# Shift and weight of the first LayerNorm moved behind the transposes of a two-layer decoder trunk

## Chip, cores and metric

One core of a Trainium2 chip. The metric is device time in microseconds of one execution, as the median of several runs. All arithmetic is float32; products are made of two-part splits of float32 (below).

## What is computed

512 tokens of width 2048 pass two layers, each followed by a LayerNorm of the residual sum:

```
x1  = layer_norm(alpha * x  + s5_mixer(x),  ln_g[0], ln_b[0])
kv  = shared_kv(x1)
out = layer_norm(alpha * x1 + nsa_mixer(x1, kv), ln_g[1], ln_b[1])

def layer_norm(x, g, b):
    mu, var = mean(x), mean((x - mu)**2)          # over the 2048 channels of a token
    return (x - mu) * rsqrt(var + 1e-5) * g + b
```

The change is in how `x1` comes from layer 0 to layer 1. `x1` is needed twice: transposed (channels on the partitions, for every projection of layer 1) and as it is (the residual of the last LayerNorm).

## The kernel before

Every float32 operand of a matmul is split into a rounded high part and a rest (`split`: a copy on ScalarE, a subtraction on VectorE), and a product is three matmuls: high by high, high by rest, rest by high (`mm3`, lines 235 to 237). Weights come in units of 512 KB through SP's queue, in the order of use, and are split ahead of their use by `Weights` (ScalarE line 78, VectorE line 85, or GpSimd line 85 for the units in `pool_units`).

The phases are: layer 0 (`layer0_in`), its output projection with the first LayerNorm and the turn (`project_out` with `turn=True`), layer 1's projections and attention (`layer1_in`), and the output projection with the second LayerNorm (`project_out` with `turn=False`). One instruction stream for each engine is written by hand; there is no scheduler. Work beside the matmuls is written as generators in a `Background`: each `yield n` says how many ticks later its next piece may be issued, and each `mm3` of the main loop is three ticks in layer 0's projection (1.5 in the first projections of layer 1).

The tokens are four tiles `t` of 128. In `project_out`, the last column step goes tile by tile, 24 matmuls of 512 columns each. When a tile's last product is done, `add` (lines 939 and 940) adds the residual and takes statistics, and `finish(t)` normalises the tile's four blocks of 128x512:

- lines 950 to 968: mean and variance, a square root on ScalarE, one Newton step on VectorE (instructions of one column).
- by the table `LN_HOW`, a block is "d" (VectorE, lines 958 and 971, two operations with the broadcast weight `gb` and shift `bb`), "p" (ScalarE line 976, then weight and shift on GpSimd, lines 977 and 978) or "m" (VectorE 958, ScalarE 973, GpSimd 974).
- line 992 stores the finished tile to DRAM as `x1_d`, the later residual.
- lines 998 to 1002: per block, four transposes on TensorE into `tp` (two buffers), a copy to `x1h` on ScalarE, a subtraction to `x1l` on VectorE.

After it, still in `project_out`, the first two projections of layer 1 start with half of the tokens (tiles 0 and 1) while tiles 2 and 3 are still turned, then do the other half; line 1065 copies their results to `first`. The four weight units of these projections are split on GpSimd.

Of the kernel before, what the change touches and what calls it, by code (L numbers as in the profile page):

```python
# [891 lines left out]
def project_out(c, sc, u0, steps, K, yh, yl, prep, x_res, ln_g, ln_b, x_out, turn):  # L892
# [54 lines left out]
    fg = FG[turn]  # L947

    def finish(t):
# [3 lines left out]
        vs, gs, bs = ([z[:, cc * 512:cc * 512 + 512] for cc in range(4)] for z in (v[:, t], gb, bb))  # L953
        how = LN_HOW[turn][t]
        late = []
        early = [cc for cc in range(4) if how[cc] != "p"]
        for i, cc in enumerate(early):
            V.scalar_tensor_tensor(vs[cc], vs[cc], mv[:, t, 0:1], gs[cc], OP.subtract, OP.mult)  # L958
            if i % 2:
                yield fg[0]  # L960
            if i == (len(early) - 1 if turn else 1):

                V.reciprocal(r, r)
                V.tensor_scalar(q, mv[:, t, 1:2], LN_EPS, r, OP.add, OP.mult)
                V.tensor_scalar(q, q, r, -0.5, OP.mult, OP.mult)
                V.tensor_scalar(r, q, 1.5, r, OP.add, OP.mult)
                if "p" in how:
                    V.tensor_scalar(nb, mv[:, t, 0:1], r, -1.0, OP.mult, OP.mult)
        for cc in sorted(range(4), key=lambda cc: "pmd".index(how[cc])):
            if how[cc] == "d":  # L970
                V.scalar_tensor_tensor(vs[cc], vs[cc], r, bs[cc], OP.mult, OP.add)
            elif how[cc] == "m":
                S.activation(vs[cc], vs[cc], AF.Copy, scale=r)
                P.tensor_tensor(vs[cc], vs[cc], bs[cc], OP.add)
            else:
                S.activation(vs[cc], vs[cc], AF.Identity, scale=r, bias=nb)
                P.tensor_tensor(vs[cc], vs[cc], gs[cc], OP.mult)
                P.tensor_tensor(vs[cc], vs[cc], bs[cc], OP.add)
            if not turn:
                o = x_out[t, :, cc * 512:cc * 512 + 512]  # L980
                if how[cc] == "d":
                    SP.dma_start(o, vs[cc])
                elif POUT:
                    P.dma_start(o, vs[cc])
                else:
                    late.append((o, vs[cc]))
            yield fg[1]
        if not turn:
            for o, z in late:
                SP.dma_start(o, z)  # L990
            return
        SP.dma_start(x_out[t], v[:, t])
        yield fg[2]
        ts = slice(t * 128, t * 128 + 128)
# [648 lines left out]
```

## Time and profile before

| | us |
|---|---|
| median of three runs (1800.74 to 1807.41) | 1804.71 |
| the profiled execution | 1800.29 |
| its span on the core | 1798.4 |
| TensorE busy in the span | 1744.9 |
| VectorE, ScalarE, GpSimd busy | 1002.6, 604.8, 177.3 |

Times in the rows are microseconds from the span's start. Engines are PE (TensorE), PEld (its weight loads), DVE (VectorE), ACT (ScalarE), POOL (GpSimd) and SP (SyncE, which only issues DMAs). In a row of a timeline stand start, duration, engine, line, operation, result<-inputs and size; xN joins N instructions that follow each other, and a bracket tells how long the engine had been idle before and what released it.

### The profile page before, as it was taken

Reading aid. Unit: us, or ns where it says so; the run is one execution under the profiler, and the core shown is the slowest. Engines: PE = TensorE matmul, PEld = TensorE weight load, DVE = VectorE, ACT = ScalarE, POOL = GpSimd, SP = SyncE. Lnnn points to the kernel's source line nnn. Section 1 sums busy time; section 2 is a strip of 40 time slices with the busy share of each in tenths; the row PEclk is TensorE's granted clock in tenths of the full one; section 3 lists DMA queues with packets and bytes.
Section 4 is the critical chain, followed back from the end, with each engine's and each line's share of the span. In section 5 each row is a group of like instructions: output and inputs, shape, how many; then the busy total and the mean of one; then the engine's idle time right before and its main releaser. Section 6 shows DMA issues by size and latency. Waiting matters only on the chain.

```text
span 1798.4 us, 21845 instructions
## 1 busy us (share of the span) xinstructions
PE 1744.9 (97%) x8455; PEld 1448.5 (81%) x8455; DVE 1002.6 (56%) x1815; ACT 604.8 (34%) x1018; POOL 177.3 (10%) x233
## 2 busy tenths in 40 slices
PE   8899998997999999999999999999999999999997
PEld 6678887886788888888888888888888888888886
DVE  7678865548333455653555553555543555665346
ACT  3344434314333333332333332333332333333120
POOL 4911100006000000000000000000000000010000
PEclk9899999999999999999999999999999999999999
DMA  6477874544233322222222222222222222236343
GB/s 227 137 191 197 214 175 133 198 142 154 88 118 117 106 80 79 77 88 82 89 76 83 81 83 94 88 77 88 72 87 94 88 77 83 77 128 231 122 140 105
DMA packets 89752, 209.70 MB, mean 117 GB/s; under 512 B 25265, under 2 KB 34721, under 8 KB 88625
## 3 DMA queue, kind: packets, MB, share of 16 engines
q1 hardware_dynamic: 81008, 181.31, 31.1%
q0 software_dynamic: 6336, 22.81, 5.2%
q10 hardware_dynamic: 2304, 4.20, 0.6%
q8 instruction: 66, 1.08, 0.3%
q14 instruction: 38, 0.30, 0.1%
HBM read 188.42 MB, written 19.86 MB: 116 GB/s over the span
## 4 chain that ended last, share of the span: by engine, by line
PE 81%; DVE 3%; ACT 1%; issue 0%; DVEq 0%; ACTq 0%
PE ps L235 23%; PE ps L237 23%; PE ps L236 23%; PE tp L1447 2%; PE s L237 1%; PE s L235 1%; PE s L236 1%; PE o L236 1%; PE o L237 1%; DVE v L958 1%; PE o L235 1%; PE cps L1212 1%; PE tp L1412 0%; PE o L1421 0%; DVE x1l L1002 0%
## 5 line engine op out<-in xcount | busy, mean ns | idle before, releaser
L235 PE MATMUL ps<-x1h,hl 128*128 128x512 f32 (+1 forms) x1440 | 563.7, 391 | 1.6 <-ACT hl L78 1.6
L237 PE MATMUL ps<-x1h,hl 128*128 128x512 f32 (+1 forms) x1440 | 556.7, 387 | 0.5 <-DVE hl L85 0.5
L236 PE MATMUL ps<-x1l,hl 128*128 128x512 f32 (+1 forms) x1440 | 555.7, 386 | 0.0
L85 DVE TENSOR_TENSOR hl<-wr,hl 128x1024 fp32r<-128x1024 f32 (+1 forms) x247 | 301.0, 1222 | 312.2 <-ACT hl L78 308.2
L78 ACT CAST hl<-wr 128x1024 fp32r<-128x1024 f32 (+1 forms) x273 | 284.4, 1045 | 220.4 <-PE ps L237 182.6
L237 PEld LDWEIGHTS ps<-x1h,hl 128*128 128x128 f32 x1440 | 270.5, 188 | 57.2 <-DVE hl L85 1.0
L235 PEld LDWEIGHTS ps<-x1h,hl 128*128 128x128 f32 x1440 | 271.0, 188 | 48.3 <-ACT hl L78 1.8
L236 PEld LDWEIGHTS ps<-x1l,hl 128*128 128x128 f32 x1440 | 271.1, 188 | 46.3
L1384 ACT ACTIVATE p<-s,m 128x384 f32<-128x384 f32 (+3 forms) x128 | 67.6, 528 | 357.6 <-DVE m L1383 357.6
L1320 POOL TENSOR_TENSOR y<-y,z 128x512 f32<-128x512 f32 x32 | 41.5, 1296 | 999.8 <-DVE z L1319 863.0
L241 DVE TENSOR_TENSOR pl<-tp,ph 128x512 fp32r<-128x512 f32 (+3 forms) x128 | 61.9, 487 | 110.0 <-ACT ph L240 109.6
L237 PE MATMUL ps<-xh,hl 128*128 128x512 f32 x256 | 104.0, 406 | 11.4 <-DMA hl<-w_in_b 11.4
L235 PE MATMUL ps<-xh,hl 128*128 128x512 f32 x256 | 109.8, 429 | 5.4 <-ACT xh L787 5.4
L236 PE MATMUL ps<-xl,hl 128*128 128x512 f32 x256 | 103.5, 404 | 2.6 <-DVE xl L788 2.6
L240 ACT CAST ph<-tp 128x512 fp32r<-128x512 f32 (+3 forms) x128 | 54.0, 426 | 151.2 <-PE tp L1447 150.9
L235 PE MATMUL ps<-hl,y1h 128*128 128x512 f32 x256 | 99.7, 389 | 0.0
L236 PE MATMUL ps<-hl,y1h 128*128 128x512 f32 x256 | 99.6, 389 | 0.0
L237 PE MATMUL ps<-hl,y1l 128*128 128x512 f32 x256 | 99.6, 389 | 0.0
L237 PEld LDWEIGHTS ps<-xh,hl 128*128 128x128 f32 x256 | 50.1, 196 | 23.9 <-DMA hl<-w_in_b 12.6
L1383 DVE TENSOR_REDUCE m<-s 128x1 f32<-128x384 f32 (+3 forms) x128 | 62.8, 491 | 4.4
L1306 DVE SCALAR_TENSOR_TENSOR z<-z,ps 128x512 f32<-128x512 f32 x48 | 33.0, 687 | 57.1 <-ACT z L1305 57.0
L235 PEld LDWEIGHTS ps<-xh,hl 128*128 128x128 f32 x256 | 50.3, 197 | 16.1 <-ACT xh L787 5.6
(350 smaller groups left out, 2306.8 us busy)
## 6 DMA issues: line engine op xcount, KB each, us to landing
wr<-b_w_in SPq DMA_DIRECT2D x128, 512.0 KB, 3.2
wr<-kv_w SPq DMA_DIRECT2D x48, 512.0 KB, 3.2
wr<-b_w_out SPq DMA_DIRECT2D x32, 512.0 KB, 3.4
wr<-w_in_b SPq DMA_DIRECT2D x24, 512.0 KB, 5.1
hl<-w_in_b POOLq DMA_DIRECT2D x22, 512.0 KB, 7.1
wr<-w_out SPq DMA_DIRECT2D x16, 512.0 KB, 3.6
xr<-xT SPq DMA_DIRECT2D x16, 256.0 KB, 4.3
Tz<-k_d SPq DMA_DIRECT2D x64, 64.0 KB, 4.2
```

The lines of the kernel that those rows point to most:

```text
L78: self.nc.scalar.copy(h[:, :n], r[:, :n])
L85: eng.tensor_tensor(l[:, :n], r[:, :n], h[:, :n].bitcast(F32), OP.subtract)
L235: PE.matmul(o, sh, mh, start=start, stop=False)
L236: PE.matmul(o, sh, ml, start=False, stop=False)
L237: PE.matmul(o, sl, mh, start=False, stop=stop)
L240: self.nc.scalar.copy(h, src)
L241: self.nc.vector.tensor_tensor(l, src, h.bitcast(F32), OP.subtract)
L1306: self.nc.vector.scalar_tensor_tensor(z, z, 1.0, ps, OP.add, OP.mult)
L1320: P.tensor_tensor(y[0], y[0], z, OP.add)
L1383: self.nc.vector.tensor_reduce(m[:, b - 1, i:i + 1], s, AX.X, OP.max, negate=True)
L1384: self.nc.scalar.activation(self.p[h, b][i], s, AF.Exp, bias=m[:, b - 1, i:i + 1], accum_out=self.sums[h, b][:, i:i + 1])
L1447: PE.transpose(tp[:, 128 * (i - j):128 * (i - j) + 128], p[i][:, at:at + 128], ident)
```

## The change

The normalised tile is made without weight and shift: (x - mean) / deviation, two blocks on VectorE and two on ScalarE, nothing on GpSimd. It is transposed in this form, and as a row of the transposed tile is one channel, weight and shift are then one number per partition. Each of the four 128x128 pieces of a block gets them on its way from `tp` into a new tile `xt` (three buffers): pieces 0 and 2 on ScalarE, 1 and 3 on VectorE. The split into `x1h` and `x1l` reads `xt`. The store to DRAM goes to a new tensor `xn_d` and holds the normalised tile; a new generator `residual`, in the fourth lane of the next phase, loads it block by block through GpSimd's queue, multiplies and adds on GpSimd, and stores it to `x1_d`. The gaps of the generators change as well.

```diff
         with yscope, ExitStack() as sc:
             xh, xl = project_out(c, sc, index["w_out"], OUT0, KE, yh, yl, lambda k: None, A["x"], A["ln_g"][0],
-                                 A["ln_b"][0], x1_d, True)
+                                 A["ln_b"][0], xn_d, True)
         with ExitStack() as sc:
-            y = layer1_in(c, sc, seq, xh, xl, y_d)
+            y = layer1_in(c, sc, seq, xh, xl, y_d, xn_d, x1_d)
...
-    gb = st.tile([128, D], F32, name="gb")
-    bb = st.tile([128, D], F32, name="bb")
-    P.dma_start(gb, ln_g.partition_broadcast(128))
-    P.dma_start(bb, ln_b.partition_broadcast(128))
+    if turn:
+        gbT = st.tile([128, 2, KD], F32, name="gbT")
+        P.dma_start(gbT, c.A["ln0"])
...
+    def finish_turn(t):
+        V.bn_aggr(mv[:, t], stats[:, t])
+        r, q, nb = (rs[:, t, i:i + 1] for i in range(3))
+        S.activation(r, mv[:, t, 1:2], AF.Sqrt, bias=eps)
+        inverse(t)
+        V.tensor_scalar(nb, mv[:, t, 0:1], r, -1.0, OP.mult, OP.mult)
+        vs = [v[:, t, cc * 512:cc * 512 + 512] for cc in range(4)]
+        ts = slice(t * 128, t * 128 + 128)
+        for cc in range(4):
+            if LN_ACT[cc]:
+                S.activation(vs[cc], vs[cc], AF.Identity, scale=r, bias=nb)
             else:
-                S.activation(vs[cc], vs[cc], AF.Identity, scale=r, bias=nb)
-                P.tensor_tensor(vs[cc], vs[cc], gs[cc], OP.mult)
-                P.tensor_tensor(vs[cc], vs[cc], bs[cc], OP.add)
...
+                V.tensor_scalar(vs[cc], vs[cc], mv[:, t, 0:1], r, OP.subtract, OP.mult)
+        yield TG[0]
         for cc in range(4):
             tp = pt.tile([128, 4, 128], F32, name="tp")
             for i in range(4):
                 PE.transpose(tp[:, i], vs[cc][:, i * 128:i * 128 + 128], ident)
+            x = st.tile([128, 4, 128], F32, tag="xt", name="xt", bufs=3)
+            for i in range(4):
+                g, b = (gbT[:, j, 4 * cc + i:4 * cc + i + 1] for j in range(2))
+                if i in XT_ACT:
+                    S.activation(x[:, i], tp[:, i], AF.Identity, scale=g, bias=b)
+                else:
+                    V.tensor_scalar(x[:, i], tp[:, i], g, b, OP.mult, OP.add)
             h, l = (z[:, 4 * cc:4 * cc + 4, ts] for z in (xh, xl))
-            S.copy(h, tp)
-            yield fg[3]
-            V.tensor_tensor(l, tp, h.bitcast(F32), OP.subtract)
+            S.copy(h, x)
+            yield TG[1]
+            V.tensor_tensor(l, x, h.bitcast(F32), OP.subtract)
             turned[t] += 1
+        SP.dma_start(x_out[t], v[:, t])
...
-FG = {True: (9, 1, 9, 6), False: (4, 3)}
-LN_HOW = {True: ('pddp', 'dppd', 'mdmm', 'dmmm'), False: ('dddd', 'dddd', 'dddd', 'dddd')}
+FG = (4, 3)
+TG = (6, 6)
+LN_ACT = (0, 1, 0, 1)
+XT_ACT = (0, 2)
...
+def residual(c, pool, xn_d, x1_d):
+    P = c.nc.gpsimd
+    for half in range(2):
+        g, b = (pool.tile([128, 1024], F32, tag=n, name=n) for n in ("g0", "b0"))
+        hs = slice(half * 1024, half * 1024 + 1024)
+        P.dma_start(g, c.A["ln_g"][0][hs].partition_broadcast(128))
+        P.dma_start(b, c.A["ln_b"][0][hs].partition_broadcast(128))
+        for t in range(4):
+            for i in range(2):
+                cs, here = (slice(lo, lo + 512) for lo in (half * 1024 + i * 512, i * 512))
+                x = pool.tile([128, 512], F32, tag="xn", name="xn", bufs=2)
+                P.dma_start(x, xn_d[t, :, cs])
+                yield RGAP
+                P.tensor_tensor(x, x, g[:, here], OP.mult)
+                P.tensor_tensor(x, x, b[:, here], OP.add)
+                P.dma_start(x1_d[t, :, cs], x)
+                yield RGAP
+RGAP = 18
...
     at.kc_tiles(0, cp)
+    bg.add(3, residual(c, cp, xn_d, x1_d))
```

How the instructions stand. First ScalarE from the first transposed block of tile 0 on, before; `tp_N` is a block's transposes in the order of their numbers, and a bracket names the engines whose semaphores the instruction waits for:

```order
L1000 CAST x1h_2744<-tp_3251 128x4x128 [waits PE_49]
L976 ACTIVATE v_2732<-v_2732,rs_2735 128x512 [waits DVE_49]
L1000 CAST x1h_2744<-tp_3272 128x4x128 [waits PE_49]
L976 ACTIVATE v_2732<-v_2732,rs_2735 128x512
L1000 CAST x1h_2744<-tp_3289 128x4x128 [waits PE_49]
```

And in the changed kernel, the first two blocks (lines of the changed file: 987 a piece, 991 the copy to `x1h`):

```order
L987 ACTIVATE xt_3218<-tp_3213,gbT_2729 128x128 [waits DMASW4_49,PE_49]
L987 ACTIVATE xt_3218<-tp_3213,gbT_2729 128x128 [waits DVE_49]
L991 CAST x1h_2743<-xt_3218 128x4x128 [waits DVE_49]
L987 ACTIVATE xt_3236<-tp_3231,gbT_2729 128x128 [waits DMASW5_49,PE_49]
L987 ACTIVATE xt_3236<-tp_3231,gbT_2729 128x128 [waits DVE_49]
L991 CAST x1h_2743<-xt_3236 128x4x128 [waits DVE_49]
```

The copy that waited for TensorE alone is now the last of three, and two of the three wait for VectorE.

VectorE of the changed kernel, from the end of tile 0's third block over the start of tile 1 (947 and 948 are the add and the statistics, 959 to 970 the one-column steps, 977 a normalised block, 989 a piece, 993 the subtraction to `x1l`):

```order
L993 TENSOR_TENSOR x1l_2744<-xt_3254,x1h_2743 128x4x128 [waits Activation_49]
L989 TENSOR_SCALAR xt_3272<-tp_3267,gbT_2729 128x128 [waits Activation_49] x2
L947 SCALAR_TENSOR_TENSOR v_2731<-xr_3148,ps_3155 128x512 [waits DMAHW0_49]
L948 BN_STATS stats_2732<-v_2731 128x6 [waits DVE_49]
L966 BN_AGGR mv_2733<-stats_2732 128x2 [waits DVE_49]
L959 RECIPROCAL rs_2734<-rs_2734 128x1 [waits Activation_49]
...
L970 TENSOR_SCALAR rs_2734<-mv_2733,rs_2734 128x1 [waits DVE_49]
L977 TENSOR_SCALAR v_2731<-v_2731,mv_2733,rs_2734 128x512 x2
L993 TENSOR_TENSOR x1l_2744<-xt_3272,x1h_2743 128x4x128
L989 TENSOR_SCALAR xt_3304<-tp_3299,gbT_2729 128x128 [waits Activation_49] x2
```

Each piece on VectorE waits for ScalarE's piece ahead of it, and tile 1's add, statistics and normalising now stand behind the pieces of tile 0's fourth block. Before, the same add stood ahead of the first `x1l` of tile 0:

```order
L971 SCALAR_TENSOR_TENSOR v_2732<-v_2732,rs_2735,bb_2729 128x512
L939 SCALAR_TENSOR_TENSOR v_2732<-xr_3149,ps_3156 128x512 [waits DMAHW0_49,PE_49]
L940 BN_STATS stats_2733<-v_2732 128x6 [waits DVE_49]
L950 BN_AGGR mv_2734<-stats_2733 128x2 [waits DVE_49]
L958 SCALAR_TENSOR_TENSOR v_2732<-v_2732,mv_2734,gb_2728 128x512 [waits DVE_49]
```

It waited for its product and for nothing of tile 0 behind the normalising.

## Rows read from the trace of the kernel before

**Rows 1.** The page's first part: busy us of each engine, its share of the span, instructions.

```profile
PE 1744.9 (97%) x8455; PEld 1448.5 (81%) x8455; DVE 1002.6 (56%) x1815; ACT 604.8 (34%) x1018; POOL 177.3 (10%) x233
```

**Rows 2.** Waits of TensorE between 404 and 470 us: what waited, for what, us in total, times, longest.

```profile
PE tp L998 <- DVE x1l L1002: 3.5, 2, 2.0
PE tp L998 <- DVE v L971: 2.6, 1, 2.6
PE tp L998 <- DVE rs L963: 2.0, 1, 2.0
PE tp L998 <- POOL v L978: 1.1, 1, 1.1
```

**Rows 3.** Busy time of the engines in stretches of 10 us: PE, PEld, DVE, ACT, POOL, each with its instructions; then TensorE's granted clock, the DMA engines' share, GB/s.

```profile
410.00:420.00 10.00, 8.85 (x47) 6.74 (x46) 9.63 (x17) 3.94 (x7) 8.91 (x7) 1.00 0.25 105
420.00:430.00 10.00, 6.54 (x38) 5.07 (x37) 9.73 (x15) 5.18 (x8) 8.50 (x5) 1.00 0.46 161
430.00:440.00 10.00, 6.61 (x55) 6.23 (x53) 9.90 (x9) 4.33 (x8) 9.28 (x5) 1.00 0.30 101
440.00:450.00 10.00, 8.76 (x74) 8.61 (x75) 5.74 (x12) 4.66 (x9) 4.07 (x3) 1.00 0.73 263
```

**Rows 4.** Timeline, tile 0 from its add to the last of the one-column steps, and tile 1's add.

```profile
404.15 0.69 DVE L939 SCALAR_TENSOR_TENSOR v<-xr,ps 128x512 f32<-128x512 f32 x1 [1.79 <-PE ps L237]
405.60 0.26 DVE L950 BATCH_NORM_AGGREGATE mv<-stats 128x2 f32<-128x24 f32 x1
405.90 0.29 ACT L952 ACTIVATE rs<-mv,eps 128x1 f32<-128x1 f32 x1 [12.01 <-DVE mv L950]
407.23 0.15 DVE L963 RECIPROCAL rs<-rs 128x1 f32<-128x1 f32 x1
408.17 0.21 DVE L968 TENSOR_SCALAR rs<-mv,rs 128x1 f32<-128x1 f32 x1
409.77 0.69 DVE L939 SCALAR_TENSOR_TENSOR v<-xr,ps 128x512 f32<-128x512 f32 x1
```

**Rows 5.** Timeline, TensorE and ScalarE around a block's transposes.

```profile
412.26 0.66 PE L998 MATMUL tp<-ident,v 128*128 128x128 f32 x4 [1.12 <-POOL v L978]
412.67 0.48 PE L235 MATMUL ps<-hl,yh 128*128 128x512 f32 x1
412.95 0.59 ACT L1000 CAST x1h<-tp 128x512 fp32r<-128x512 f32 x1 [1.13 <-PE tp L998]
414.49 0.48 PE L235 MATMUL ps<-hl,yh 128*128 128x512 f32 x1
```

**Rows 6.** Groups of VectorE's instructions, shapes kept apart: line, operation, result<-inputs, size, count, then busy us, mean ns of one, idle before.

```profile
L1436 DVE TENSOR_SCALAR p<-p,r 128x512 f32<-128x512 f32 x32 | 15.4, 481 | 0.0
L1436 DVE TENSOR_SCALAR p<-p,r 128x128 f32<-128x128 f32 x32 | 9.2, 287 | 1.1
L241 DVE TENSOR_TENSOR pl<-tp,ph 128x128 fp32r<-128x128 f32 x32 | 9.2, 287 | 27.4 <-ACT ph L240 27.4
L241 DVE TENSOR_TENSOR yl<-sig,yh 128x512 fp32r<-128x512 f32 x8 | 5.5, 693 | 5.5 <-ACT yh L240 5.5
L966 DVE TENSOR_SCALAR rs<-rs 128x1 f32<-128x1 f32 x8 | 1.7, 214 | 0.3
L958 DVE SCALAR_TENSOR_TENSOR v<-v,mv,gb 128x512 f32<-128x512 f32 x28 | 28.7, 1066 | 0.3
```

**Rows 7.** The same of ScalarE.

```profile
L240 ACT CAST ph<-tp 128x128 fp32r<-128x128 f32 x32 | 8.6, 268 | 36.7 <-PE tp L1447 36.7
L553 ACT ACTIVATE B1s<-B,sg 128x128 f32<-128x128 f32 x8 | 3.2, 401 | 2.4 <-DVE B L548 2.4
L976 ACT ACTIVATE v<-v,rs 128x512 f32<-128x512 f32 x4 | 3.2, 813 | 4.2 <-DVE rs L968 4.2
L787 ACT CAST xh<-xr 128x512 fp32r<-128x512 f32 x16 | 9.9, 618 | 19.7 <-DMA xr<-xT 19.7
L78 ACT CAST hl<-wr 128x1024 fp32r<-128x1024 f32 x271 | 283.2, 1048 | 215.8 <-PE ps L237 182.6 <-issue 12.3 <-DMA wr<-b_w_out 7.6
```

**Rows 8.** Timeline, line 958 on VectorE without and with GpSimd at work.

```profile
405.90 1.41 DVE L958 SCALAR_TENSOR_TENSOR v<-v,mv,gb 128x512 f32<-128x512 f32 x2
411.52 2.92 DVE L958 SCALAR_TENSOR_TENSOR v<-v,mv,gb 128x512 f32<-128x512 f32 x2
412.16 1.74 POOL L977 TENSOR_TENSOR v<-v,gb 128x512 f32<-128x512 f32 x1
```

**Rows 9.** Timeline, the last two blocks' transposes and the second copy to `first`, which waits for the last of the 96 matmuls of the second half.

```profile
448.76 1.21 PE L998 MATMUL tp<-ident,v 128*128 128x128 f32 x8
461.51 0.58 ACT L1065 COPY first<-ps 128x512 f32<-128x512 f32 x1 [5.17 <-PE ps L237]
```

**Rows 10.** For the residual's new way: DMA issues (count, KB each, median us to landing), GpSimd's addition in layer 1, and the first exponential over 256 columns of layer 1.

```profile
xr<-x_d SPq DMA_DIRECT2D x16, 256.0 KB, 3.2
raw<-bc POOLq DMA_DIRECT2D x8, 256.0 KB, 7.7
gb<-ln_g POOLq DMA_DIRECT2D x2, 1024.0 KB, 8.9
L1320 POOL TENSOR_TENSOR y<-y,z 128x512 f32<-128x512 f32 x32 | 41.5, 1296 | 999.8 <-DVE z L1319 863.0 <-DVE pc L1366 136.7
621.04 0.48 ACT L1384 ACTIVATE p<-s,m 128x256 f32<-128x256 f32 x1 [2.24 <-DVE m L1383]
```

More of the change, by code (lines that the diff above doesn't have):

```diff
@@ L210, in emit @@
         y_d = dram.tile([NH, 128, T], F32, name="y_d")
+        xn_d = dram.tile([4, 128, D], F32, name="xn_d")
         with ExitStack() as sc:
@@ L910, in project_out @@
             W.extra[u1 + 1 + i] = (st, "x", 2)
-    gb = st.tile([128, D], F32, name="gb")
-    bb = st.tile([128, D], F32, name="bb")
-    P.dma_start(gb, ln_g.partition_broadcast(128))
-    P.dma_start(bb, ln_b.partition_broadcast(128))
+    if turn:
+        gbT = st.tile([128, 2, KD], F32, name="gbT")
+        P.dma_start(gbT, c.A["ln0"])
+    else:
+        gb = st.tile([128, D], F32, name="gb")
+        bb = st.tile([128, D], F32, name="bb")
+        P.dma_start(gb, ln_g.partition_broadcast(128))
+        P.dma_start(bb, ln_b.partition_broadcast(128))
     v = st.tile([128, 4, D], F32, name="v")
@@ L930, in load_res @@
             xr = st.tile([128, 512], F32, tag="xr", name="xr", bufs=n_res)
-            SP.dma_start(xr, x_res[t, :, cc * 512:cc * 512 + 512])
+            cs = slice(cc * 512, cc * 512 + 512)
+            SP.dma_start(xr, x_res[t, :, cs])
             res[cc, t] = xr
@@ L946, in project_out, with inverse @@
     turned = [0] * 4
-    fg = FG[turn]
-    def finish(t):
+    def inverse(t):
+        r, q = rs[:, t, 0:1], rs[:, t, 1:2]
+        V.reciprocal(r, r)
+        V.tensor_scalar(q, mv[:, t, 1:2], LN_EPS, r, OP.add, OP.mult)
+        V.tensor_scalar(q, q, r, -0.5, OP.mult, OP.mult)
+        V.tensor_scalar(r, q, 1.5, r, OP.add, OP.mult)
+    def finish_turn(t):
         V.bn_aggr(mv[:, t], stats[:, t])
@@ L952, in finish @@
         S.activation(r, mv[:, t, 1:2], AF.Sqrt, bias=eps)
[L953 to L973, printed above, removed]
-                P.tensor_tensor(vs[cc], vs[cc], bs[cc], OP.add)
-            else:
-                S.activation(vs[cc], vs[cc], AF.Identity, scale=r, bias=nb)
-                P.tensor_tensor(vs[cc], vs[cc], gs[cc], OP.mult)
[L978 to L994, printed above, removed]
+        inverse(t)
[5 more added lines that the diff above has]
+                S.activation(vs[cc], vs[cc], AF.Identity, scale=r, bias=nb)
+            else:
+                V.tensor_scalar(vs[cc], vs[cc], mv[:, t, 0:1], r, OP.subtract, OP.mult)
@@ L998, in finish @@
                 PE.transpose(tp[:, i], vs[cc][:, i * 128:i * 128 + 128], ident)
+            x = st.tile([128, 4, 128], F32, tag="xt", name="xt", bufs=3)
[3 more added lines that the diff above has]
+                    S.activation(x[:, i], tp[:, i], AF.Identity, scale=g, bias=b)
+                else:
+                    V.tensor_scalar(x[:, i], tp[:, i], g, b, OP.mult, OP.add)
             h, l = (z[:, 4 * cc:4 * cc + 4, ts] for z in (xh, xl))
-            S.copy(h, tp)
-            yield fg[3]
-            V.tensor_tensor(l, tp, h.bitcast(F32), OP.subtract)
+            S.copy(h, x)
+            yield TG[1]
+            V.tensor_tensor(l, x, h.bitcast(F32), OP.subtract)
             turned[t] += 1
+        SP.dma_start(x_out[t], v[:, t])
+    def finish(t):
+        V.bn_aggr(mv[:, t], stats[:, t])
+        r = rs[:, t, 0:1]
+        S.activation(r, mv[:, t, 1:2], AF.Sqrt, bias=eps)
+        vs, gs, bs = ([z[:, cc * 512:cc * 512 + 512] for cc in range(4)] for z in (v[:, t], gb, bb))
+        for cc in range(4):
+            V.scalar_tensor_tensor(vs[cc], vs[cc], mv[:, t, 0:1], gs[cc], OP.subtract, OP.mult)
+            if cc % 2:
+                yield FG[0]
+            if cc == 1:
+                inverse(t)
+        for cc in range(4):
+            V.scalar_tensor_tensor(vs[cc], vs[cc], r, bs[cc], OP.mult, OP.add)
+            SP.dma_start(x_out[t, :, cc * 512:cc * 512 + 512], vs[cc])
+            yield FG[1]
     bg = Background(4, True)
@@ L1009, in done @@
         if cc == 3:
-            bg.add(t, finish(t))
+            bg.add(t, (finish_turn if turn else finish)(t))
             bg.advance(t)
@@ L1619, in layout @@
         "ln_g": ln_g,
+        "ln0": np.stack([a[0].reshape(KD, 128).T for a in (ln_g, ln_b)], 1),
         "ln_b": ln_b,
```

3 lines of the change are left out of this document (1 added, 2 removed).

## The prediction

> **What bounds the kernel now.** I began with the page's first part: TensorE is busy for 1744.9 us, 97% of the span [rows 1]. A change that adds and removes no matmul can win only where TensorE stands still, so the next view was TensorE's waits around the turn. There are five, 9.2 us in all, every one at a block's transposes, released by VectorE or by GpSimd [rows 2]. The windows give the same sum another way: between 410 and 450 us TensorE is busy for 8.85 + 6.54 + 6.61 + 8.76 of 40, so it is idle for 9.2 us, at a granted clock of 1.00 [rows 3]. In the first 30 of these VectorE is busy for 9.6 to 9.9 of each 10: the turn is bound by VectorE. Why it is so full stands in the rows of line 958: two of them take 1.41 us with GpSimd idle and 2.92 beside GpSimd's line 977 [rows 8]. Over its 28 instructions that is 28.7 - 28 x 0.705 = 9.0 us of stretching [rows 6].
>
> The most the turn can give back is therefore 9.2 us, 0.51% of the time. A measurement of this kernel can tell about 0.5% (9.0 us) from no change, so a clear gain needs nearly all of it.
>
> **What is removed.** GpSimd's fourteen operations on the blocks, and with them the stretching; two loads of 1 MB (`gb`, `bb`), whose place is long before the turn and which delayed nothing that I can find; VectorE's second pass over a block. The transposes, the matmuls and the store's place on SP's queue keep their number and order, so TensorE's own work costs nothing more. The second `project_out` issues the same instructions as before.
>
> **What is added: a chain.** The order rows of the changed kernel show what the diff alone does not. The four pieces of a block write one tile `xt`, and each waits for the piece before: ScalarE, VectorE, ScalarE, VectorE, then ScalarE's copy, then VectorE's subtraction. Two short queues that look parallel run as one. And the next tile's add stands on VectorE behind the last pieces of this tile, where before it waited for its product alone. So norm and turn of a tile, and then the next tile, follow each other without overlap. I price one link after the other.
>
> - Add to first normalised block. The aggregate ends at 405.86, the square root at 406.19; the one-column steps took 407.23 to 408.38, 1.15 us; the add began at 404.15 [rows 4]. A block of 512 on VectorE without a weight costs 0.48 [rows 6]. Hence 406.19 + 1.15 + 0.48 = 407.82, which is 3.67 us after the add.
> - Transposes to their result: 412.26 to 412.95, 0.69 [rows 5].
> - A piece on VectorE: no such row; 0.29 from the subtraction out of `tp` and the in-place multiplication, both 128x128 [rows 6]. Its lower end is a one-column instruction, 0.21 [rows 6].
> - A piece on ScalarE: no such row. The cast of 128x128 out of `tp`, without scale and shift, takes 0.27; scale and shift from memory cost 0.81 - 0.62 = 0.19 on a block, and a 128x128 with one of them takes 0.40 [rows 7]. I take 0.44, between 0.40 and 0.27 + 0.19 = 0.46; the ends are 0.27 and 0.50.
> - ScalarE's copy, now from `xt`: 0.62 [rows 7]. VectorE's subtraction: 0.70 as that of `yl`, which also reads two tiles [rows 6].
> - A passage between engines: aggregate 405.86 to square root 405.90, 0.035 [rows 4].
>
> The Trainium skill ("ScalarE: Activation LUTs", Rules for kernel authors) budgets about 0.3 us for an ACTIVATE with a bias pointer and 0.83 ns per element: an estimate of 0.41 for 128 columns. With 0.41 in place of 0.44 the sum below would be about 0.5 us lower. No row here shows the form itself.
>
> **The sum.** First block of a tile: four pieces and three passages, 1.57 us. Each later block: copy 0.62, subtraction 0.70, pieces 0.29 + 0.44 + 0.29 (its first piece on ScalarE runs beside the subtraction), five passages of 0.035: 2.52 us. A tile's period is 3.67 + 0.69 + 1.57 + 3 x 2.52 = 13.5 us. TensorE has for a tile 24 matmuls, 5.6 us by the distance of two adds [rows 4], and four groups of transposes at 1.82 - 6 x 0.235 = 0.42 each (six matmuls and a group lie between 412.67 and 414.49 [rows 5]): 7.3 us. The chain is longer than TensorE's work by 6.2 us a tile.
>
> The adds then come at 404.15, 417.6 and 431.1. Between tile 2's four blocks ScalarE has three weight casts queued, 1.05 us each [rows 7], in places where it would wait only 0.29 for VectorE: 3 x 0.76 = 2.3 us. So tile 3's add is at 446.9 and its first transposes at 450.6. Behind them TensorE has 81 matmuls of 256 columns and the rest of the transposes, 81 x 0.12 + 4 x 0.42 = 11.4 us, where 0.12 is 96 such matmuls in 449.97 to 461.51 [rows 9]; then the second half, 11.5 us. That half ends at 473.5 instead of 461.5: **+12.0 us**. The same by waits: tile 0's first transposes now stand six matmuls behind the product and wait 3.67 - 1.41 = 2.3; the two following tiles 6.2 each; tile 3, with the casts, about 8.1; together 22.8, less the 9.2 that go: +13.6. I take +12.8.
>
> Bounds. A ScalarE piece of 0.27 takes 0.17 x 5 pieces x 3.5 tiles = 3.0 off, and a VectorE piece of 0.21 another 1.5 to 2.5: +7. A ScalarE piece of 0.50 adds 1. The subtraction now reads two tiles in memory, while GpSimd still splits the four weight units of the projections; the stretching that the pair of line 958 showed, doubling [rows 8], on four subtractions would add 2.8: +16 to +17. After the turn nothing gives time back, since TensorE has no gap of that size there.
>
> The profiled execution took 1800.29, 4.4 below the median of 1804.71, which is the base: 1804.7 + 12.8 = **1817.5 us**.
>
> **Rivals.**
>
> *A, the other side: VectorE freed of GpSimd makes the turn fit under TensorE.* The Trainium skill ("SBUF — State Buffer", Who interferes with whom) says that VectorE and GpSimd share a port pair as an exclusive lock, held for a whole instruction; the trace agrees in that 1.41 became 2.92 [rows 8]. By rows alone: the 9.0 us of stretching go [rows 6]. If then nothing but VectorE's own work counted, a tile would cost it add and aggregate 0.95, statistics some 0.5, one-column steps 1.15 [rows 4], two blocks 0.96, eight pieces 2.3 and four subtractions 2.8 [rows 6]: 8.7 us, 1.4 over TensorE's 7.3. The waits would be 2.3 + 3 x 1.4 = 6.5, which is 2.7 under the 9.2 of before: 1802.0. It decides if the period is below 7.3 + 2.3 = 9.6. Against it: it wants perfect overlap, and the waits in the order rows forbid just that. Chance 0.05.
>
> *B: the pieces of a block run side by side.* If the waits between pieces cost nothing because each engine's two pieces go in one run, a block costs ScalarE 0.62 + 0.88 = 1.5 and VectorE 0.70 + 0.58 = 1.28, under the 1.82 that TensorE takes for six matmuls and a group. The period is 3.67 + 0.69 + 0.8 + 3 x 1.82 = 10.6, 2.9 less than in the forecast, over 3.5 tiles 10 us: +2.5, or 1807. For it: the two engines write different columns of `xt`. Against: every second piece has a wait for the other engine in the order rows. Chance 0.15.
>
> *C: the residual comes late and holds up attention.* It takes 16 blocks through GpSimd's queue in order: a load of 256 KB, 3.2 us as SP's of `xr`, and two operations of 1.3: 5.8 us, 93 in all [rows 10]. From 474 on, with two pairs of broadcast loads of 8.9 [rows 10], it ends at about 585. The first exponential over 256 columns waits for these DMAs; it was at 621.04 [rows 10], now at 633.5. The slack is 48 us, 3.0 a block, so a load of over 6.2 us decides. GpSimd's own loads of `raw`, same size, take 7.7 [rows 10]: 16 x 4.5 - 48 = 24 us more, 1841. Against: 3.2 is the row of the very same shape. Issuing itself, for which I have no row, takes 16 off the slack of 48 for each us of it in a block. GpSimd's keys and positions for layer 1 queue behind these blocks as well, which a mean block of 5.8 hides and one of 10 does not. Chance 0.12.
>
> **How the numbers follow.** The chain as priced gets 0.68, A 0.05, B 0.15, C 0.12. The chain's own range is 1811 to 1823 (+7 to +17, and 1 or 2 for the base). B pulls the low end to 1806; C beyond 1828 and A are left out, together less than 2 in 10. A clear gain would need more than A gives: 0.02. Within 9.0 us of before lie most of A, B and the chain's lowest corner, 0.04 + 0.15 + 0.09: 0.28. Slower: 0.70.
>
> **What would show it.** Tiles' adds on VectorE some 13.5 us apart, where they were 5.6; TensorE idle for about 22 us between 404 and 475, all at transposes, released by ScalarE or VectorE at the normalised block; the last copy to `first` at 473 to 476 instead of 461.5; pieces of about 0.44 on ScalarE and 0.29 on VectorE in strict turns; the later phase shifted by the same 12 to 13 us and no more. I am wrong if pieces of one block overlap, if the period is near 7 to 10 us, or if the exponential waits for the residual.

## The result and the profile after

The changed kernel takes 1824.69 us (median of 4 runs, 1823.33 to 1825.90) beside 1806.06 for the kernel before: a ratio of 1.0119, interval 1.0098 to 1.0140, or 18 to 25 us; the two medians alone would give 1.0103, 18.6 us. The forecast was +12.8. The kernel before varies more from run to run than the changed one (1797.69 to 1808.93 beside the experiments, with medians of 1800.76 to 1802.88), and three of its four runs here lie in the upper half of that, so 18.6 us is probably too small. The profiled executions differ by 23.0 (1823.33 and 1800.29), their spans by 22.9 (1821.3 and 1798.4), and it is these that the rows below divide up.

TensorE's waits between 400 and 485 us (what waited, for what, us in total, times, longest) and the 10 us stretches (columns as in [rows 3]):

```profile
PE tp L982 <- DVE v L977: 20.9, 4, 7.2
```

```profile
410.00:420.00 10.00, 7.03 (x32) 5.39 (x30) 6.02 (x12) 5.19 (x11) 0.00 (x0) 0.84 0.23 93
430.00:440.00 10.00, 4.18 (x16) 3.23 (x15) 6.45 (x18) 5.24 (x10) 0.00 (x0) 0.81 0.00 0
450.00:460.00 10.00, 4.92 (x23) 4.95 (x24) 6.84 (x15) 5.34 (x10) 5.48 (x8) 0.50 0.68 223
460.00:470.00 10.00, 10.00 (x86) 10.00 (x85) 4.36 (x9) 4.03 (x9) 2.71 (x5) 1.00 0.42 163
```

In place of the five waits of [rows 2], 9.2 us, stand four of 20.9, each for the normalised block of a tile, as the chain has it. VectorE, 9.6 to 9.9 of 10 busy in [rows 3], is now busy for 4.5 to 6.8 of each 10 us between 410 and 460, and ScalarE for 5.2 to 7.2: two engines idle for 3 to 5 of each 10 us, and TensorE waits for them. New is the clock: 1.00 throughout in [rows 3], here down to 0.50.

The chain itself, the second block of tile 0 on ScalarE and VectorE (timeline), from the first block's copy to its own:

```profile
410.64 0.62 ACT L991 CAST x1h<-xt 128x512 fp32r<-128x512 f32 x1 [0.48 <-DVE xt L989]
411.29 0.69 DVE L993 TENSOR_TENSOR x1l<-xt,x1h 128x512 fp32r<-128x512 f32 x1 [0.69 <-ACT x1h L991]
411.60 0.46 ACT L987 ACTIVATE xt<-tp,gbT 128x128 f32<-128x128 f32 x1 [0.34 <-PE tp L982]
412.09 0.41 DVE L989 TENSOR_SCALAR xt<-tp,gbT 128x128 f32<-128x128 f32 x1
412.54 0.46 ACT L987 ACTIVATE xt<-tp,gbT 128x128 f32<-128x128 f32 x1 [0.48 <-DVE xt L989]
413.03 0.41 DVE L989 TENSOR_SCALAR xt<-tp,gbT 128x128 f32<-128x128 f32 x1 [0.53 <-ACT xt L987]
413.48 0.62 ACT L991 CAST x1h<-xt 128x512 fp32r<-128x512 f32 x1 [0.48 <-DVE xt L989]
```

Each instruction begins when the other engine's ends; only the first piece, at 411.60, waits for its transposes beside the subtraction, which makes this block 2.84 us long where the next two take 2.63 and 2.64. The tiles' adds on VectorE and the two copies to `first`:

```profile
404.09 0.69 DVE L947 SCALAR_TENSOR_TENSOR v<-xr,ps 128x512 f32<-128x512 f32 x1 [1.94 <-PE ps L239]
418.63 0.68 DVE L947 SCALAR_TENSOR_TENSOR v<-xr,ps 128x512 f32<-128x512 f32 x1
433.61 0.68 DVE L947 SCALAR_TENSOR_TENSOR v<-xr,ps 128x512 f32<-128x512 f32 x1
450.41 0.68 DVE L947 SCALAR_TENSOR_TENSOR v<-xr,ps 128x512 f32<-128x512 f32 x1
474.75 0.59 ACT L1073 COPY first<-ps 128x512 f32<-128x512 f32 x1 [7.35 <-PE ps L239]
480.47 0.59 ACT L1073 COPY first<-ps 128x512 f32<-128x512 f32 x1 [5.13 <-PE ps L239]
```

The last copy, at 461.51 in [rows 9], is 19.0 us later. The first one was at 455.76 before the change:

```profile
455.76 0.59 ACT L1065 COPY first<-ps 128x512 f32<-128x512 f32 x1 [5.17 <-PE ps L237]
```

Tile 3's first transposes and what comes behind them on TensorE:

```profile
455.08 1.09 PE L982 MATMUL tp<-ident,v 128*128 128x128 f32 x4 [7.15 <-DVE v L977]
455.82 0.56 PE L237 MATMUL ps<-x1h,hl 128*128 128x256 f32 x1
456.18 0.41 PE L238 MATMUL ps<-x1l,hl 128*128 128x256 f32 x1
456.39 0.41 PE L239 MATMUL ps<-x1h,hl 128*128 128x256 f32 x1
```

After 7.15 us of standing still the transposes take 1.09 for 0.66 [rows 5], and a matmul of 256 columns follows the last after 0.21 instead of 0.12: the lower of the clock's two levels (1.2 GHz), up to about 460.

### The profile page after: what moved, and what is told of

Read it like the earlier page. It is cut to its first block, busy times and chain, and to the rows that moved or that the text cites. A ratio compares the mean times of both kernels' runs of the same rounds, so it can differ in the third digit from the quotient of the medians.

```text
span 1821.3 us, 21949 instructions
## 1 busy us (share of the span) xinstructions
PE 1754.3 (96%) x8455; PEld 1455.4 (80%) x8455; DVE 1009.0 (55%) x1839; ACT 619.1 (34%) x1048; POOL 221.2 (12%) x286
## 4 chain that ended last, share of the span: by engine, by line
PE 81%; DVE 2%; ACT 2%; issue 0%; DVEq 0%; ACTq 0%
PE ps L237 23%; PE ps L239 23%; PE ps L238 23%; PE tp L1457 2%; PE s L239 1%; PE s L237 1%; PE s L238 1%; PE o L238 1%; PE o L239 1%; PE o L237 1%; PE cps L1222 1%; DVE xt L989 0%; ACT xt L987 0%; PE tp L1422 0%; PE tp L982 0%; ACT hl L78 0%
## 5 line engine op out<-in xcount | busy, mean ns | idle before, releaser
L85 DVE TENSOR_TENSOR hl<-wr,hl 128x1024 fp32r<-128x1024 f32 (+1 forms) x247 | 310.2, 1260 | 314.9 <-ACT hl L78 310.8
L237 PEld LDWEIGHTS ps<-xh,hl 128*128 128x128 f32 x256 | 49.4, 193 | 15.9 <-ACT xh L789 5.6
```

The lines of the kernel that those rows point to most:

```text
L85: eng.tensor_tensor(l[:, :n], r[:, :n], h[:, :n].bitcast(F32), OP.subtract)
L237: PE.matmul(o, sh, mh, start=start, stop=False)
```

## The experiments

The starts of tile 0's add differ from run to run by up to 4.6 us, for reasons ahead of the turn, so places in the turn are given from that add on. "First copy" is the first of the two copies to `first`: 51.6 us behind the add before the change, 70.7 after it. Each time stands beside the kernel before on the same chip. Where two runs' intervals overlap, the argument goes by the places, and each of these comes from one profiled execution.

**One engine.** All pieces on ScalarE, all blocks normalised on VectorE:

```diff
-LN_ACT = (0, 1, 0, 1)
-XT_ACT = (0, 2)
+LN_ACT = (0, 0, 0, 0)
+XT_ACT = (0, 1, 2, 3)
```

> All 32 pieces on VectorE move to ScalarE, and all normalised blocks to VectorE; the sum of the work on a block stays about the same. Theory 1 (the turn is one chain through both engines, and the next tile's add stands behind the last pieces): add, statistics and aggregate (1.65 us) now run beside ScalarE's pieces, the rest stays one chain: 0.69 + 4 x (4 x 0.46 + 0.62 + 0.05) + 0.33 + 1.2 + 0.54 = 12.8 us from one tile's first transposes to the next, where the changed kernel has 14.5 and 15.0 (tile 3: about 16.5 for 17.6, with the weight casts). Tile 3's first transposes at about 450.5 for 455.1, second copy to first at about 475.5 for 480.5, about 1819.5 us. Rival (the alternation itself, a passage between engines for every piece, is what costs; 3 passages a block, 48 in all): gain of 6 us or more within the blocks, blocks at about 2.0 us each. Rival (VectorE's load is the bound, as before the change): freeing VectorE of its pieces brings the period to about 10 us, second copy below 468, 1812 us.

Measured: 1817.99 beside 1801.80, 1.0082 (1.0053 to 1.0111). The adds are 12.78, 12.54 and 14.43 apart (14.5, 15.0, 16.8 in the changed kernel), the first copy at 65.9, the waits 15.7 us. The period is theory 1's 12.8, but that is luck, since its terms are not: where nothing holds ScalarE up, a block takes 2.06 us and not 2.51, which is the first rival's price.

```profile
413.44 1.51 ACT L987 ACTIVATE xt<-tp,gbT 128x128 f32<-128x128 f32 x4 [1.03 <-PE tp L982]
415.51 1.50 ACT L987 ACTIVATE xt<-tp,gbT 128x128 f32<-128x128 f32 x4
417.57 1.50 ACT L987 ACTIVATE xt<-tp,gbT 128x128 f32<-128x128 f32 x4
```

Part of that gain is lost again, since ScalarE now waits for transposes, 1.03 us here, behind TensorE at its lower clock (0.85 between 410 and 420). The next tile's norm still stands in the chain.

**No pieces.** The loop over the four pieces and its tile `xt` go, and copy and subtraction read `tp`:

```diff
...
-            S.copy(h, x)
+            S.copy(h, tp)
...
-            V.tensor_tensor(l, x, h.bitcast(F32), OP.subtract)
+            V.tensor_tensor(l, tp, h.bitcast(F32), OP.subtract)
```

> Leaves out weight and shift on the transposed side: copy and subtraction read tp directly. Theory 1 (the loss is the pieces' place in the chain): the chain of a tile is then add to first transposes only, 3.65 us, beside 1.41 us of matmuls; waits of 2.3 us four times, 9 us in all as before the change; the granted clock stays at 1.00; second copy to first at 461 to 463 for 480.5, about 1807 us (2 us above before, from the residual's work on GpSimd beside the next phase). Rival (the norm's one-column steps and the order of the adds cost as much as the pieces): waits of over 15 us left, 1815 us or more.

Measured: 1808.58 beside 1801.80, 1.0032 (1.0017 to 1.0048). First copy at 56.3; waits 2.5, 2.0, 2.0 and 4.5 us, 11.1 in all. The pieces carry 14.4 of the 19.0 us that the turn lost. That the clock stays at 1.00 was wrong: it was 0.87 behind the first wait and 0.66 behind the last, which is longer because tile 3's square root stands on ScalarE behind a weight cast that waits for its load.

**Residual later.**

```diff
     P = c.nc.gpsimd
+    yield RSTART
...
-RGAP = 18
+RGAP = 16
+RSTART = 48
```

> Residual starts 48 ticks (about 11 us) later in the next phase and goes on with smaller gaps (16 for 18); nothing else. Theory 1a (GpSimd's first products of the residual stretch VectorE's split of a weight unit at 483 us, the wait of 0.98 for 0.53 us lets the granted clock fall to 0.81 for some 5 us, 2.1 us in all): the wait is back at about 0.5, clock 1.00 between 481 and 491, shift against before stays at 19.0 through the phase instead of 21.1: 1822.6 us. Rival (the fall comes from what happened in the turn, not from the residual): the wait or the clock stays, no change from 1824.7.

Measured: 1821.31 beside 1801.80, 1.0103 (1.0074 to 1.0131), not to be told from the changed kernel's 1.0119. The edit did not do what it was meant to: GpSimd's first product stands 70.6 us behind tile 0's add, for 70.1. A gap sets where an instruction stands among the others of the program; but GpSimd's queue holds only the residual and a few DMA issues here, so its products still begin when their loads are in. What changed is who comes first, in the changed kernel and then in this run:

```profile
481.35 1.27 POOL L1496 TENSOR_TENSOR xn<-xn,g 128x512 f32<-128x512 f32 x1 [3.04 <-DMA xn<-xn_d]
482.03 3.91 DVE L85 TENSOR_TENSOR hl<-wr,hl 128x1024 fp32r<-128x1024 f32 x2 [13.91 <-ACT hl L78]
```

```profile
479.37 3.45 DVE L85 TENSOR_TENSOR hl<-wr,hl 128x1024 fp32r<-128x1024 f32 x2 [13.59 <-ACT hl L78]
479.62 2.12 POOL L1497 TENSOR_TENSOR xn<-xn,g 128x512 f32<-128x512 f32 x1 [3.11 <-DMA xn<-xn_d]
```

With VectorE's split ahead, the wait for it is 0.5 us again, but the clock between 480 and 490 is 0.83, and the shift against before still grows from 16.3 to 17.8 us there. So the longer wait is 0.45 us and no condition of the lower clock, which costs the larger part. Whether the residual has a part in that fall, this run can't tell, since it is still there. In *Warm* it stands in nearly the same place (its second block 1.6 us behind the last copy, 1.8 here), and the clock stays at 1.00.

**Warm.** `yh` times `yh` into the transposes' buffer ahead of the first block:

```diff
+            for _ in range(WARM[t] if cc == 0 else 0):
+                PE.matmul(tp.rearrange("p a b -> p (a b)"), yh[:, 0, 0:128], yh[:, 1], start=True, stop=True)
...
+WARM = (0, 19, 20, 25)
```

> Before the first transposes of tiles 1, 2 and 3, TensorE does 19, 20 and 25 further matmuls of 512 columns into the transposes' own buffer, which the transposes then overwrite: it works through most of the three long waits (4.5, 4.7 and 5.9 of 5.4, 5.8 and 7.2 us). Theory 1b (the waits cost a second time, because TensorE's granted clock falls to its lower level in them and the matmuls and transposes behind them run at half speed for 3 to 5 us): clock 1.00 from 420 to 480, transposes of tile 1's first block 0.6 to 0.7 for 1.09, tile 3's first transposes 1 to 2 us earlier, second copy 4 to 5 us earlier (476), about 1820 us. Rival (the lower clock only stands beside the waits, the chain on ScalarE and VectorE sets the end either way): second copy within 1 us of 480.5, 1824.7 us.

Measured: 1820.67 beside 1801.80, 1.0096 (1.0064 to 1.0128), too wide to tell it from the changed kernel's 1.0119; the trace tells more. Its windows:

```profile
420.00:430.00 10.00, 8.12 (x43) 6.10 (x41) 6.18 (x16) 5.46 (x11) 0.00 (x0) 1.00 0.25 105
450.00:460.00 10.00, 8.29 (x64) 7.63 (x64) 6.93 (x17) 5.90 (x11) 4.28 (x7) 1.00 0.74 258
```

With 64 useless matmuls in the waits the clock is at 1.00 from 420 on, the first copy at 67.6 for 70.7, 3 us where I expected 4 to 5, and nothing is lost at the start of the next phase either: 16.1 us behind before there, counted from the add, for 21.1. By these two traces the clock is 3.0 us of the loss in the turn; of the further 2 at the start of the next phase, 0.45 are the wait for the split, 0.5 here as well. That the matmuls in the turn are what keeps the clock up there is not shown: behind the same two waits, 1.6 us for the cast and 0.5 for the split, it reads 0.83 in *Residual later* and in both runs of *18 ticks*, the second of which had 1.00 throughout the turn, and 1.00 in the kernel before and six other runs, among them *Ahead only*, whose turn had 0.66. The first transposes of tile 3 come only 0.7 earlier (50.2 for 51.0 behind the add): the chain hardly notices, the work behind it does.

**Norm ahead.** The edit of *One engine*, and

```diff
-TG = (6, 6)
+TG = (27, 6)
```

> As the run with all pieces on ScalarE, and the first transposes of a tile 27 ticks instead of 6 behind its product, so that the next tile's add, statistics, square root and normalising stand ahead of this tile's pieces on both engines. Theory 1 (the turn costs because norm and pieces of consecutive tiles form one chain): the chain is cut, ScalarE's own work is what is left, 4 x (4 x 0.46 + 0.62) + 0.29 = 10.1 us a tile where the other run had 12.5 to 12.8; ready some 53 to 54 us behind tile 0's add, second copy 62 + 5 (lower clock) behind the first tile's add at most, where the changed kernel has 76.4 and the kernel before 57.4: about 1812 us. Rival (the period is set by the sum of the pieces' work whatever the order): second copy within 2 us of that run (71.7 behind tile 0's add), 1818 us.

Measured: **1797.95 beside 1801.12, 0.9981 (0.9963 to 0.9999)**; the first copy at 48.6, 3.0 us ahead of the kernel before the change; waits 5.6 us and 0.5 for a split on GpSimd; clock 1.00. The gain in time is at the edge of what these runs can tell. Far better than I expected, and the reason is in ScalarE's rows, as it was already in *One engine*:

```profile
408.77 1.49 ACT L987 ACTIVATE xt<-tp,gbT 128x128 f32<-128x128 f32 x4
410.29 0.63 ACT L991 CAST x1h<-xt 128x512 fp32r<-128x512 f32 x1
410.82 1.50 ACT L987 ACTIVATE xt<-tp,gbT 128x128 f32<-128x128 f32 x4
412.35 0.62 ACT L991 CAST x1h<-xt 128x512 fp32r<-128x512 f32 x1
```

Four pieces in a row take 1.50 us, not 4 x 0.46: with nothing to wait for, one begins before the last has ended. A block is 2.06 us where I counted 2.46, and the next tile's norm runs beside it.

**Half by rows.** Blocks 0 and 2 with weight and shift on VectorE before the transposes, blocks 1 and 3 on ScalarE behind them, the gaps of before; the core of it:

```diff
+        for cc in (1, 3):
+            S.activation(vs[cc], vs[cc], AF.Identity, scale=r, bias=nb)
+        for cc in (0, 2):
+            V.scalar_tensor_tensor(vs[cc], vs[cc], r, bs[cc], OP.mult, OP.add)
```

> A version that should beat both: blocks 0 and 2 of each tile get weight and shift on VectorE before the transposes as before (two operations of 0.70 without GpSimd beside them), blocks 1 and 3 on ScalarE alone behind the transposes; gaps as before the change; GpSimd does nothing in the turn but the weight splits; the residual's later part covers only blocks 1 and 3. Theory (VectorE's load without GpSimd's stretching, 3.1 + 2.8 + 2.8 = 8.7 us a tile, ScalarE 8.0, each independent of the other): waits of TensorE 4 to 6 us instead of 9.2, clock 1.00, second copy 53 to 55 behind tile 0's add (57.4 before), 3 to 5 us faster than before. Rival (ScalarE's blocks of 4 x 0.46 + 0.62 are late for TensorE's 1.82 between groups of transposes): waits stay at 9 or more, same time as before or up to 5 us slower.

Measured: 1802.04 beside 1801.12, 0.9991 (0.9977 to 1.0006): no difference. The waits are 7.1 us, between the two theories, and the clock falls to 0.78 behind the longest, 4.3 us, which is VectorE's, beside GpSimd's weight splits (the first of them and VectorE's rows):

```profile
422.53 2.63 POOL L85 TENSOR_TENSOR hl<-wr,hl 128x1024 fp32r<-128x1024 f32 x1 [90.25 <-ACT hl L78]
422.82 2.89 DVE L1004 TENSOR_TENSOR x1l<-xt,x1h 128x512 fp32r<-128x512 f32 x1
425.64 2.83 DVE L985 SCALAR_TENSOR_TENSOR v<-v,rs,bb 128x512 f32<-128x512 f32 x1
428.39 0.68 DVE L1004 TENSOR_TENSOR x1l<-tp,x1h 128x512 fp32r<-128x512 f32 x1
428.99 2.29 DVE L1004 TENSOR_TENSOR x1l<-xt,x1h 128x512 fp32r<-128x512 f32 x1
```

**The kernel before without GpSimd's part of the turn.**

```diff
                 S.activation(vs[cc], vs[cc], AF.Copy, scale=r)
-                P.tensor_tensor(vs[cc], vs[cc], bs[cc], OP.add)
...
-                P.tensor_tensor(vs[cc], vs[cc], gs[cc], OP.mult)
-                P.tensor_tensor(vs[cc], vs[cc], bs[cc], OP.add)
```

> The kernel before without GpSimd's 14 operations in the turn; it leaves out weight and shift of the blocks that GpSimd gave them, and changes nothing else. The prediction's premise (all of TensorE's 9.2 us of waiting is VectorE stretched by GpSimd, 9.0 us): line 958 at 0.70 each throughout, waits at most 2.5 us, second copy 50 to 51 behind tile 0's add (57.4), 6 to 7 us faster than before. Rival (VectorE is full by its own work, the stretching hid in gaps): waits of 6 or more, under 3 us faster.

Measured: 1799.38 beside 1801.12, 0.9985 (0.9971 to 0.9999). First copy 2.4 earlier than in the kernel before, waits 4.7, and the clock at 0.74 between 420 and 430, behind a wait of 4.0. One pair on VectorE against one weight split on GpSimd:

```profile
419.85 5.55 DVE L958 SCALAR_TENSOR_TENSOR v<-v,mv,gb 128x512 f32<-128x512 f32 x2
```

```profile
419.72 2.39 POOL L85 TENSOR_TENSOR hl<-wr,hl 128x1024 fp32r<-128x1024 f32 x1 [88.21 <-ACT hl L78]
422.29 2.56 POOL L85 TENSOR_TENSOR hl<-wr,hl 128x1024 fp32r<-128x1024 f32 x1 [0.18 <-ACT hl L78]
```

The two operations, 1.4 us by themselves, last as long as the two splits and 0.6 more. The splits stretch VectorE as the 14 operations did, so my 9.0 us of stretching are not all the change's to remove. The time goes by the rival (under 3 us faster), the waits lie between the two theories: about 2 to 3 us were there.

**Ahead only.** `TG = (27, 6)`, the pieces in turns as in the change.

> The other half of the run that won: the first transposes 27 ticks behind the product, but the pieces in turns on both engines as in the changed kernel. Theory 1c (two things multiply: in turns a block costs the chain 2.64 us, on one engine in a row 2.06; and only with VectorE free of pieces can the next norm run beside them): the order alone leaves the pieces' chain of 4 x 4 x 2.64 = 42 us with the norms of tiles 2 and 3 between them, first copy 64 to 67 behind tile 0's add (70.6 in the changed kernel, 65.9 with one engine alone, 48.6 with both), 1818 us. Rival (the order alone did it): first copy at 55 or earlier, 1806 us.

Measured: 1816.88 beside 1800.76, 1.0084 (1.0062 to 1.0107), first copy at 64.8, as theory 1c had it. So of the 22 us between the changed kernel and the run *Norm ahead*, the winner, one engine alone gives 4.7, the order alone 5.9, both together 22.0. "One engine" includes the normalising, all of it on VectorE; no run has that apart.

**Pairs.** `XT_ACT = (0, 1)`, all else the change's.

> The changed kernel with pieces 0 and 1 on ScalarE and 2 and 3 on VectorE: the same instructions on the same engines, one passage between them instead of three. Theory 1c (pieces of one engine in a row overlap: 1.50 us for four on ScalarE where each alone takes 0.46; in turns each pays its whole duration and a passage): a block costs about 2.3 us instead of 2.64, about 1.3 us a tile; first copy 66 to 67 behind tile 0's add for 70.6, about 1820 us. Rival (a piece costs 0.46 or 0.41 however it stands): blocks stay above 2.55 us, first copy within 1.5 of 70.6.

Measured: 1818.39 beside 1800.76, 1.0093 (1.0070 to 1.0116), first copy at 67.0. Adds 13.76 and 13.71 apart; a block is 2.18 us (ScalarE's copies at 412.95 and 415.13):

```profile
412.95 0.62 ACT L991 CAST x1h<-xt 128x512 fp32r<-128x512 f32 x1 [0.85 <-DVE xt L989]
413.48 0.80 ACT L987 ACTIVATE xt<-tp,gbT 128x128 f32<-128x128 f32 x2
415.13 0.62 ACT L991 CAST x1h<-xt 128x512 fp32r<-128x512 f32 x1 [0.85 <-DVE xt L989]
```

Two pieces take 0.80 on ScalarE and 0.73 on VectorE: taking turns cost 0.46 us a block with no instruction more. ScalarE still stands idle for 0.85 us until VectorE's pair is done. These waits are there because the pieces write one tile; no run gave each engine a tile of its own, so whether the two would then run side by side stays open.

**18 ticks, and a block on VectorE.** The winner with `TG = (18, 6)`; then this with the fourth block's pieces on VectorE (`XT_ACT = (0, 1, 2)`, now counting blocks):

```diff
-                if i in XT_ACT:
+                if cc in XT_ACT:
```

> The run that won (all pieces on ScalarE, norm ahead) with its first transposes 18 instead of 27 ticks behind the product. Theory (ScalarE's row of pieces, busy from 408.8 to 447.1 with hardly a gap, sets when the second half can start): it starts 2 us earlier and so ends 1 to 2 us earlier; first copy 47 behind tile 0's add for 48.6; 1 to 2 us faster than that run, 4 to 5 faster than before. Rival (the square root of the next tile now stands behind two blocks' pieces, and the norm is late again): waits above the 5.6 of that run, no gain or a loss.

> As the run with 18 ticks, and each tile's fourth block gets its four pieces on VectorE instead of ScalarE. Theory (ScalarE is the bound, VectorE idle for a third): ScalarE loses 6 us of work in the turn, VectorE gains some 5.5; TensorE's waits fall to 2 or 3, first copy 45 to 46 behind tile 0's add, 2 us faster than the run with 18 ticks. Rival (a block on the other engine brings back a passage and queues the pieces behind the next tile's add and norm, as in the changed kernel): waits of 6 or more, slower than the run with 18 ticks.

Measured: 1799.85 beside 1800.76, 0.9982 (0.9967 to 0.9997), first copy at 49.4; and 1803.72 beside 1800.76, 1.0014 (0.9999 to 1.0028), first copy at 53.4. With 18 ticks the rival held in its result, no gain, and in its mechanism, since the first transposes wait for the norm again (3.1 us); but the waits at transposes are 4.4 us in all, not above 5.6, and the clock falls to 0.94 and 0.89. With the block on VectorE the rival held: the transposes wait 5.2 us for VectorE's pieces, 9.8 in all.

**No split on GpSimd.** The winner with `OPOOL = ()`, the list of the weight units that GpSimd splits.

> The fastest run (all pieces on ScalarE, norm 27 ticks ahead) with the four weight units of the next projections split on VectorE instead of GpSimd, so that GpSimd does nothing in the turn. Theory (what is left of GpSimd's lock still costs: three subtractions and a normalising beside its splits took 1.7 to 1.9 and 2.9 us for 0.69 and 1.9, some 3.3 us, and TensorE waits 1.8 us for the last subtraction of tile 1 and 0.5 for a split): subtractions back at 0.69, these two waits below 0.7 together, first copy 47 behind tile 0's add for 48.6, 1 to 2 us faster than that run. Rival (four splits of 1.25 us on VectorE cost as much as the stretching they end): first copy within 0.7 us of 48.6, no difference.

Measured: 1802.35 beside 1802.88, 1.0000 (0.9987 to 1.0013). The subtractions are back at 0.68, and yet the first copy is at 51.7. Neither theory had that; the rows show a third thing:

```profile
427.21 1.23 DVE L85 TENSOR_TENSOR hl<-wr,hl 128x1024 fp32r<-128x1024 f32 x1 [1.19 <-ACT hl L78]
428.36 0.68 DVE L993 TENSOR_TENSOR x1l<-xt,x1h 128x512 fp32r<-128x512 f32 x1
430.22 1.23 DVE L85 TENSOR_TENSOR hl<-wr,hl 128x1024 fp32r<-128x1024 f32 x1 [1.17 <-ACT hl L78]
431.36 0.68 DVE L947 SCALAR_TENSOR_TENSOR v<-xr,ps 128x512 f32<-128x512 f32 x1
```

A split on VectorE waits for ScalarE's cast, which stands behind ScalarE's pieces, and tile 3's add stands behind the split: 29.7 us behind tile 0's add instead of 26.2. It is the fault of the change once more, an instruction that could run queued behind one that can't.

## Why the prediction held, and where its sizes were off

- **The bound.** TensorE's waits at the transposes: yes; the window of [rows 2] holds two more, 1.6 and 0.5 us, at the start of the next phase. "The most the turn can give back is 9.2 us" stands; that all of it is the 14 operations' stretching does not (*without GpSimd's part*).
- **The chain.** The order rows were right on every link: strict turns within a block, the next add behind the last pieces. *One engine*, *Pairs* and *Ahead only* each loosen one link and win 3.7 to 5.9 us of place; *No pieces* takes it away.
- **Luck.** The chain's own range ended at 1823, and 1824.69 lies above it; the room up to 1828 was made for C, which did not come. The base helped too: 1804.71 is 2 to 4 us above the later medians of the kernel before. Two of the signs failed: the last copy is at 480.5, not at 473 to 476, and the later phase shifted by 21.1 and at the end 22.9, where I had "no more".
- **The terms.** Period 13.5 us: 14.5 and 15.0 measured. The piece on VectorE is the term that was mis-sized most: 0.29 taken from the nearest 128x128 rows, 0.41 measured; on ScalarE 0.44 taken, 0.46 measured (alone; 0.375 in a row of four). The Trainium skill's estimate of 0.41 ("ScalarE: Activation LUTs", Rules for kernel authors) lies between the two. A later block was 2.64 for 2.52, the first 1.85 for 1.57, and from tile 0's add to ScalarE's first piece it took 4.70 (404.09 to 408.79) for 4.36. And tile 3's pair of normalised blocks took 1.84 for 0.99 beside GpSimd's last split, 0.85 us that I priced on the subtractions instead, which GpSimd did not meet here:

```profile
436.75 0.99 DVE L977 TENSOR_SCALAR v<-v,mv,rs 128x512 f32<-128x512 f32 x2
452.17 2.34 POOL L85 TENSOR_TENSOR hl<-wr,hl 128x1024 fp32r<-128x1024 f32 x1 [0.99 <-ACT hl L78]
453.55 1.84 DVE L977 TENSOR_SCALAR v<-v,mv,rs 128x512 f32<-128x512 f32 x2
```

- **The sum.** Of +19.0 at the last copy, 12.0 are the chain as priced (I put 12.8 to leave room to the count by waits). In *Warm*, at full clock, tile 3's first transposes are at 50.2 behind tile 0's add; the forecast's 450.6 is 46.4. So 3.8 are the chain's sizes: 3.0 over three periods and 0.8 in tile 3's norm. 0.7 more is what the clock adds to the chain (51.0), and 2.3 what it adds behind: from those transposes to the last copy 25.4 us, for 23.1 in *Warm*; the sum had 22.9, 0.2 too little. 12.0 + 3.8 + 0.7 + 2.3 + 0.2 = 19.0. My count by waits had 8.1 for tile 3, where 6.2 + 2.3 is 8.5, and it fails for another reason: the waits grew by 11.7 only (20.9 for 9.2), and the other 7.3 us are TensorE's own work at the lower clock, of which *Warm* puts 3.0 on the path; the rest fell into time in which TensorE would have waited anyway.
- **What was missing.** I priced waits at their own length. TensorE's clock was at 1.00 through the waits of [rows 2], up to 2.6 us, and I took it to stay there. Here it fell behind waits of 2.5 to 7.2 us: 3.0 us in the turn, and most of the 2.1 at the start of the next phase, where the same 1.6 us wait stands in both kernels. There TensorE waits 0.98 for VectorE's split, for 0.53; the clock is 0.85 and 0.81 in the two halves of the 10 us from 480.5 on, 1.00 before the change. Why it falls there stays open (*Warm*). The last 1.7 us come in the last projection, where the waits are the same and the clock reads 0.83 once, for 1.00; nothing in the turn explains it, and no run settled it. The profiled executions differ by more than the medians, by 4.4 us, of which this may be part.
- **Rivals.** A did not come about, as its point of decision says: periods of 14.5, not under 9.6. Its lock is real: a row above has 2.89 for 0.69 beside a split on GpSimd. By the Trainium skill ("SBUF — State Buffer", Who interferes with whom) the one blocks for the other's whole instruction, and with 2.4 us for a split the traces agree. B was wrong for this kernel: no pieces overlap. Even in *Pairs*, where each engine's two pieces go in one run as B has it, a block takes 2.18, not 1.5. C stayed out, narrowly. The exponential over 256 columns is 21.1 us later, the shift of the phase. But a block of the residual took about 8 us, not 5.8 (loads 4.5, and 0.55 to issue each DMA), and the queue stood for 32 us behind a cast that waited for ScalarE; the last store was issued at 636.9, 5.2 us ahead of that exponential at 642.1, and such a store takes 3.1.

## What to carry to other kernels

Two engines that write pieces of one tile in turns, each waiting for the other as here, are one engine with longer instructions: give a tile's pieces to one engine in a row, and put the next tile's critical work ahead of them in both queues. Either alone gave a quarter of it; both together turned a change that cost 1.2% into one about 0.2% faster (0.0 to 0.4%). Of a moved operation, price what is queued behind it while it waits; and give a wait on TensorE an upper bound above its length, since the clock may fall behind it. Look in the trace whether an edit moved what it was to move: a gap that is only an order delays nothing on an engine with nothing else to do.
